# The first feed-forward's last output phase in three sweeps, and the next layer's token norm by halves

## The chip, the cores and the metric

The kernel runs on one core of a Trainium2 chip. The metric is the device time of one execution in microseconds, the median of several runs. The engines are named as in the profile: PE (TensorE, matmuls; PEld is its weight load), DVE (VectorE), ACT (ScalarE), POOL (GpSimd) and SP (SyncE, which issues most of the DMAs here). Each engine takes its instructions in the order in which they are written down for it.

## The reference, cut to what matters

Two layers act on 512 latent tokens and 256 context tokens of width 1024, all in fp32. Layer 0 is windowed attention and a SwiGLU feed-forward, layer 1 is retention and a feed-forward. Every mixer and every feed-forward stands behind an RMS norm whose result is scaled and shifted by numbers made from a condition vector, one set for the latent tokens and one for the context:

```
def rms_norm(x, g):
    y = xf * lax.rsqrt(jnp.mean(xf * xf, axis=-1, keepdims=True) + EPS)
    return y * g
def modulate(h, shift, scale):
    return h * (1 + scale) + shift
def swiglu(h, w_in, w_out):
    gate, up = jnp.split(h @ w_in, 2, axis=-1)
    return (jax.nn.silu(gate) * up) @ w_out

for i in range(DEPTH):                      # i = 0: attention, i = 1: retention
    h_x = modulate(rms_norm(x, norm1_g[i]), mx[0], mx[1])
    h_c = modulate(rms_norm(y_ctx, norm1_g[i]), mc[0], mc[1])
    ...                                     # the mixer, x = x + mx[2] * out_x, likewise y_ctx
    x = x + mx[5] * swiglu(modulate(rms_norm(x, norm2_g[i]), mx[3], mx[4]), ffn_w_in[i], ffn_w_out[i])
    ...                                     # likewise y_ctx with mc, in layer 0
```

The change lies where layer 0 ends and layer 1 begins: the last part of `swiglu(...) @ w_out` with its gated residual for both streams, the sums of squares of the new `x` and `y_ctx`, and `rms_norm` and `modulate` of layer 1's mixer. The hidden width of the feed-forward is 2816, that is 22 tiles of 128.

## The kernel before, in words

Activations lie with the 1024 features on the partitions, in eight tiles of 128, and tokens along the free dimension: `xr[d]` is the latent residual (128 x 512), `cres[d]` the context's (128 x 256). A matmul with a weight is done in three: weight and activation are each split into a rounded upper part and the rest (`split`, lines 164 to 166, and `next_w`, lines 136 to 142: ACT casts the upper part, DVE subtracts it for the lower), and `mm3` (lines 144 to 150) adds upper x upper, lower x upper and upper x lower in PSUM.

**The feed-forward of layer 0.** The 22 hidden tiles come in groups of 2, 4, 4, 4, 4 and 4. From the third tile on `seven` (line 1025) makes a tile by seven block products (line 908, `product`) of 12 matmuls each on sums of quarters of weights and activations: DVE forms the quarter sums of the weight pair `g`, `u` (lines 1031 to 1037), and the weights `b11`, `t1`, `b24` and `b3` are split from them. The products go to PSUM banks X, Y and Z in the order b11, b11, b24, t1, b3, b3, b24. Four of them use bank Y one after another, and ACT copies the first three out (lines 1046, 1051, 1055) before the next one on Y may start. After the first tile of a group, `output` (line 1078) multiplies the group before with its output weights: for a group of four there are four weights of 128 x 1024, each for two of the eight feature tiles `d`.

**The last output phase** is `output(prev, True)` (line 1156). It runs in two sweeps over `d`: first all eight for the latent tokens (banks `pj`, 512 columns, 12 matmuls each), then all eight for the context (bank Z, 256 columns). The four output weights stay in place for both. After each `d` comes the gated residual on DVE (`gated_add`, line 253) and the square (ACT, line 209) added to the running sum of squares (line 210, on DVE for the latent tokens, on POOL for the context). In the second `d` of the context sweep `rms(0)` (line 213) makes the latent statistics: a product with a matrix of ones (line 217), logarithm, exponential and square on ACT (lines 101, 196), two instructions on DVE (lines 197, 198).

**The start of retention.** `latent_norm` (line 1224) forms the normed and scaled latent tokens from whole rows of 512 (line 1229, DVE), and from them the upper (ACT, line 1232) and lower part (DVE, line 1233): for the feature tiles 0 to 3 only the first 256 tokens, for 4 to 7 all 512. The first value weights of head 0 are split between the two calls (lines 1326 to 1328). Then come the first value products (`values_first`, line 1266), the context statistics and norm (`context_norm`), the other value products, and `token_sums` (lines 1202 to 1215), which forms sums and differences of quarters of the normed latent tokens (`sA`) for the query, key and gate products. Before those, the key and query weights of head 0 are combined (lines 1374 to 1378) and split. The first query product is `product_q` on `sA` (line 1253).

**What sets the order.** The kernel is written as one stream of calls. A scheduler distributes it to the engines and puts each engine's instructions into one fixed order, from its own estimate of their times. Weight buffers come from pools: `w_raw` takes a raw weight from DRAM into one of two shared rooms or, by `raw_turn`, every third one into a room of the feed-forward's own pool. `w_parts` (line 126) hands out the rooms of the split weights in turn, two in the shared pool `rp` and one in the feed-forward's pool `fp`; the counter `wsel` says whose turn it is. A room is used again when its last reader is done, so the turn decides what a cast waits for. SP issues the weight loads in order, each when its room is free. In the last output phase weights one and two and the fourth take rooms by that turn from `rp`, `rp` and `fp`, and the third (`spare_w`) takes rooms that nothing else uses by then.

Of the kernel before, what the change touches and what calls it, by code (L numbers as in the profile page):

```python
# [8 lines left out]
F32 = mybir.dt.float32  # L9
# [40 lines left out]
def dit_kernel(ctx, tc, xT, cT, crow, small, consts, masks, tabs0, tabs1, jtab, adaQ, adaN, adaT, wst, out):  # L50
# [1015 lines left out]
    def square_and_stats(s, d, t):  # L1066
        add_square(s, d, t, eng=(nc.vector, nc.gpsimd)[s])
        if s == 1 and d == 1:
            ln_exp_turn()
            rms(0)  # L1070

# [6 lines left out]
    def output(acts, final):  # L1078
        gsz = len(acts)
        nd = 1024 // (gsz * P)  # L1080
        w = []

        def one(s, res, c, d):
            while len(w) * nd <= d:
                w.append(spare_w() if final and len(w) == 2 else next_w(fp, 1, raw_turn()))
            wd = w[d // nd]
            o = bank("Z")[:, 0:SC] if s else pj()
            for k in range(gsz):
                c0 = k * nd * P + (d % nd) * P
                mm3(o, (wd[0][:, c0:c0 + P], wd[1][:, c0:c0 + P]),  # L1090
                    (acts[k][:, c], acts[k][:, c.start + WIDE:c.stop + WIDE]), k == 0, k == gsz - 1)
            ins = gated_add(s, 0, 5, d, o, res)
            if cr and not final and s == 0 and d % 2:
                ada_next(ins)
            if final:
                square_and_stats(s, d, res[d])

        if final:
            for st in streams:
                for d in range(KT):  # L1100
                    one(*st, d)
        else:
            for d in range(KT):
                for st in streams:
                    one(*st, d)
# [23 lines left out]
    for gsz in FFN_GROUPS:  # L1129
        acts = []  # L1130
        for i in range(gsz):
# [4 lines left out]
            else:  # L1136
                if f == PLAIN:
                    last_sum()
                a, end = seven()
# [6 lines left out]
            if i == 0 and prev is not None:  # L1146
                output(prev, False)
# [7 lines left out]
    wsel[0] = 0  # L1155
    output(prev, True)
# [4 lines left out]
    for l, s, w in ((1, 0, 0), (1, 1, 0), (1, 0, 1)):  # L1161
        fold_gain(l, s, w)

# [60 lines left out]
    def latent_norm(ks, behind=()):  # L1224
        b, y = mods[1, 0], ssq[0]
        for k in ks:
            hm.append(t_qk(F32))
            t = hm[k]
            after(nc.vector.scalar_tensor_tensor(t, xr[k], acol[1, 0, 0][:, k:k + 1], y, mult, mult), behind)
            c = HALVES[0] if k < 4 else slice(0, SX)  # L1230
# [633 lines left out]
```

## Time and profile before

| | us |
|---|---|
| three runs | 1770.1, 1770.05, 1769.09 |
| their median | 1770.05 |
| the profiled execution | 1765.14 |
| its span, first to last instruction | 1763.4 |
| mean granted TensorE clock over the span | 0.996 of full speed |
| last output phase, latent sweep | about 858 to 881 of the span |
| last output phase, context sweep | about 881 to 893 |
| head 0 of retention up to its first query product | about 893 to 935 |

The span is what the views of the profile cover; the profiled execution's own time is 1.7 us more. The rows give the start in microseconds from the start of the span, the time, the engine, the line, the operation, and output and inputs with their shape; in square brackets stands the idle time before an instruction and what ended it. A row with a count (x3) is several instructions taken together, from the start of the first to the end of the last. Matmuls overlap, so their pace is the distance from one start to the next and not the time of one.

### The profile page before, as it was taken

Reading aid. Unit: us, or ns where it says so; the run is one execution under the profiler, and the core shown is the slowest. Engines: PE = TensorE matmul, PEld = TensorE weight load, DVE = VectorE, ACT = ScalarE, POOL = GpSimd, SP = SyncE. Lnnn points to the kernel's source line nnn. Section 1 sums busy time; section 2 is a strip of 40 time slices with the busy share of each in tenths; the row PEclk is TensorE's granted clock in tenths of the full one; section 3 lists DMA queues with packets and bytes.
Section 4 is the critical chain, followed back from the end, with each engine's and each line's share of the span. In section 5 each row is a group of like instructions: output and inputs, shape, how many; then the busy total and the mean of one; then the engine's idle time right before and its main releaser. Section 6 shows DMA issues by size and latency. Waiting matters only on the chain.

```text
span 1763.4 us, 27889 instructions
## 1 busy us (share of the span) xinstructions
PE 1716.5 (97%) x10984; PEld 1531.5 (87%) x10984; DVE 1332.7 (76%) x2342; ACT 841.3 (48%) x1487; POOL 122.4 (7%) x267
## 2 busy tenths in 40 slices
PE   6999999999999999999998999999999999999999
PEld 4788787889999999999887888898897889989998
DVE  6687786478778787877799758758767897777774
ACT  5467786364434333343464534524534565345442
POOL 0014344000000000000010000000000100000000
PEclk9999999999999999999999999999999999999999
DMA  9510014133243434343333434434433323233322
GB/s 345 232 49 14 15 58 157 49 127 113 96 132 122 142 120 155 108 145 130 96 133 120 157 98 132 155 108 133 146 105 108 96 93 111 85 108 108 97 83 84
DMA packets 60899, 205.65 MB, mean 117 GB/s; under 512 B 6752, under 2 KB 7136, under 8 KB 60640
## 3 DMA queue, kind: packets, MB, share of 16 engines
q1 hardware_dynamic: 53856, 178.71, 30.5%
q0 software_dynamic: 6912, 25.17, 4.5%
q8 instruction: 86, 1.41, 0.3%
q14 instruction: 45, 0.37, 0.1%
HBM read 201.75 MB, written 2.10 MB: 116 GB/s over the span
## 4 chain that ended last, share of the span: by engine, by line
PE 78%; DVE 12%; DMA 5%; ACT 3%; issue 1%; POOL 0%; SPq 0%; DVEq 0%; ACTq 0%; POOLq 0%
PE Y L908 14%; PE Z L908 7%; PE pj L150 7%; PE pj L149 7%; PE pj L148 7%; DMA wraw<-in_wst_dram 4%; PE X L908 3%; PE Y L1253 3%; PE Z L1266 3%; DVE wlo L166 3%; PE pO L732 2%; PE pT L704 2%; PE S L684 2%; PE pj L1266 2%; PE X L1253 1%
## 5 line engine op out<-in xcount | busy, mean ns | idle before, releaser
L165 ACT CAST whi<-wraw 128x1024 fp32r<-128x1024 f32 x177 | 185.5, 1051 | 305.2 <-PE Z L150 71.5
L166 DVE TENSOR_TENSOR wlo<-wraw,whi 128x1024 fp32r<-128x1024 f32 x177 | 216.1, 1223 | 39.4 <-ACT whi L165 38.9
L908 PE MATMUL Y<-aq,whi 128*128 128x384 f32 x640 | 173.9, 335 | 0.4 <-ACT hn L1046 0.3
L253 DVE SCALAR_TENSOR_TENSOR res<-pj,mod,res 128x512 f32<-128x512 f32 (+1 forms) x110 | 80.4, 732 | 81.2 <-PE pj L150 80.1
L141 DVE TENSOR_TENSOR wlo<-wraw,whi 128x1024 fp32r<-128x1024 f32 x79 | 96.5, 1223 | 35.2 <-ACT whi L140 34.6
L140 ACT CAST whi<-wraw 128x1024 fp32r<-128x1024 f32 x79 | 82.9, 1049 | 77.1 <-PE Z L150 24.3
L908 PEld LDWEIGHTS Y<-aq,whi 128*128 128x128 f32 x640 | 116.7, 188 | 1.8 <-ACT hn L1046 1.4
L908 PE MATMUL Y<-aq,wlo 128*128 128x384 f32 x320 | 107.0, 334 | 0.0
L271 DVE CUSTOM_DVE_ANT_0 y<-adaw,crow,small_sb 128x1024 bf16<-128x1024 f32 x64 | 81.9, 1280 | 32.9 <-DMA adaw<-in_adaT_dram 32.7
L1266 PE MATMUL Z<-whi,sA 128*128 128x512 f32 x256 | 81.0, 392 | 1.4 <-ACT whi L165 1.4
L101 ACT ACTIVATE pr<-pr,stat,qs 128x513 f32<-128x513 f32 (+2 forms) x96 | 74.2, 775 | 12.4 <-DVE stat L691 9.7
L698 POOL TENSOR_SCALAR pr<-pr,stat 128x512 f32<-128x512 f32 (+2 forms) x96 | 65.3, 693 | 76.6 <-DVE stat L695 57.7
L148 PE MATMUL pj<-ax,whi 128*128 128x512 f32 x176 | 68.7, 390 | 1.2 <-DVE res L253 1.2
L150 PE MATMUL pj<-ax,whi 128*128 128x512 f32 x176 | 68.7, 390 | 0.0
L149 PE MATMUL pj<-ax,wlo 128*128 128x512 f32 x176 | 68.5, 389 | 0.0
L148 PE MATMUL pj<-act,whi 128*128 128x512 f32 x168 | 66.0, 393 | 0.0
L149 PE MATMUL pj<-act,wlo 128*128 128x512 f32 x168 | 65.9, 392 | 0.0
L150 PE MATMUL pj<-act,whi 128*128 128x512 f32 x168 | 65.5, 390 | 0.0
L268 POOL DMA_DIRECT2D adaw<-in_adaT_dram x48 | 25.6, 533 | 514.6 <-DVE mod L271 420.1
L908 PE MATMUL Y<-sA,whi 128*128 128x256 f32 x304 | 60.8, 282 | 0.0
L908 PEld LDWEIGHTS Y<-aq,wlo 128*128 128x128 f32 x320 | 60.1, 188 | 0.0
L685 DVE CUSTOM_DVE_ANT_0 pr<-S,mask,qs 128x256 f32<-128x256 f32 (+1 forms) x96 | 52.5, 568 | 8.4 <-PE S L684 5.1
(545 smaller groups left out, 5227.8 us busy)
## 6 DMA issues: line engine op xcount, KB each, us to landing
wraw<-in_wst_dram SPq DMA_DIRECT2D x238, 512.0 KB, 3.6
adaw<-in_adaT_dram POOLq DMA_DIRECT2D x48, 512.0 KB, 3.8
wx<-in_wst_dram SPq DMA_DIRECT2D x24, 512.0 KB, 4.9
adan<-in_adaQ_dram SPq DMA_DIRECT2D x16, 512.0 KB, 8.4
adan<-in_adaN_dram SPq DMA_DIRECT2D x16, 512.0 KB, 7.5
res<-in_xT_dram SPq DMA_DIRECT2D x16, 256.0 KB, 4.4
q<-in_adaN_dram SPq DMA_DIRECT2D x16, 256.0 KB, 3.2
aq<-in_adaN_dram SPq DMA_DIRECT2D x12, 256.0 KB, 5.9
```

The lines of the kernel that those rows point to most:

```text
L101: ins = nc.scalar.activation(*args, **kw)
L140: nc.scalar.copy(hi, raw)
L141: nc.vector.tensor_tensor(lo, raw, hi, op=sub)
L148: nc.tensor.matmul(o, whi, xhi, start=first, stop=False)
L149: nc.tensor.matmul(o, wlo, xhi, start=False, stop=False)
L150: return nc.tensor.matmul(o, whi, xlo, start=False, stop=last)
L165: nc.scalar.copy(hi, t)
L166: return nc.vector.tensor_tensor(lo, t, hi, op=sub)
L253: return nc.vector.scalar_tensor_tensor(res[d], o, mods[l, s][:, part, d:d + 1], res[d], mult, add)
L271: after(nc.vector.tensor_tensor_reduce(junk, w, cr[:, s * 1024:(s + 1) * 1024], 1.0, sm_t[:, C_ADAB + l * 48 + j:C_ADAB + l * 48 + j + 1], ...
L908: nc.tensor.matmul(o, p, r, start=first and k + i == 0, stop=k == 3 and i == 2, skip_group_check=not first)
L1266: ins = nc.tensor.matmul(o, p, r, start=first and k + i == 0, stop=k == 3 and i == 2, skip_group_check=not first)
```

## The change

The last output phase goes over the eight feature tiles three times instead of twice: the first 256 latent tokens, the other 256, then the context. Each sweep has its own statistics: those of the first half are made in the second sweep, those of the second half in the third. The squares of the first half are added on DVE, all others on POOL. Each product of a sweep has 256 columns, and the products alternate between the banks `pj` and Z.

The four output weights take other rooms. The first comes by the turn, which is set so that it gets the room of the feed-forward's own pool; the second and third lie in halves in eight rooms `aq` that held the upper activations of the feed-forward (`token_room_w`); the fourth is `spare_w`. So that the turn comes out like this, `wsel` is set to 2 ahead of the last hidden tile and again ahead of the last output phase. The last hidden tile's own weights thereby change rooms too: b11 gets the room in `fp`, which the tile before used for b3, and b24 and b3 get the rooms in `rp`. The two rooms in `rp` are then free for retention's first value weights while the sweeps run.

The latent norm of retention works on halves: both calls at its old place do the first 256 tokens of all feature tiles, and a third call, ahead of `token_sums`, does the other 256, with the upper and lower part for the tiles 4 to 7.

```diff
+    def token_room_w():
+        raw, w = raw_turn(), ([], [])
+        for c in range(2):
+            hi, lo = (T(ep, 768, "aq", 8, F32R)[:, 0:512] for _ in range(2))
+            split(raw[:, 512 * c:512 * c + 512], hi, lo)
+            w[0].append(hi)
+            w[1].append(lo)
+        return w
...
-        if final:
-            for st in streams:
-                for d in range(KT):
-                    one(*st, d)
...
+    def last_output(acts):
+        w = []
+        for s, res, c, part in ((0, xr, HALVES[0], HALVES[0]), (0, xr, HALVES[1], HALVES[1]),
+                                (1, cres, slice(SX, WIDE), slice(0, SC))):
             for d in range(KT):
+                if len(w) * 2 <= d:
+                    w.append((lambda: next_w(fp, 1, raw_turn()), token_room_w, token_room_w, spare_w)[len(w)]())
+                o = bank("Z")[:, 0:SC] if d % 2 else pj(SC)
+                out_products(o, w[d // 2], d % 2 * P, acts, c, 2 * P)
+                nc.vector.scalar_tensor_tensor(res[d][:, part], o, mods[0, s][:, 5, d:d + 1], res[d][:, part],
+                                               mult, add)
+                first = s == 0 and c.start == 0
+                add_square(s, d, res[d], part, eng=nc.vector if first else nc.gpsimd, fresh=first or s == 1)
+                if not first and d == 1:
+                    if s == 0:
+                        ln_exp_turn()
+                    rms(0, HALVES[s])
...
                 if f == PLAIN:
                     last_sum()
+                if f == FT - 1:
+                    wsel[0] = 2
                 a, end = seven()
...
-    wsel[0] = 0
-    output(prev, True)
+    wsel[0] = 2
+    last_output(prev)
     F.close()
     E.close()
...
+    wsel[0] = 0
...
-    def latent_norm(ks, behind=()):
-        b, y = mods[1, 0], ssq[0]
+    def latent_norm(ks, half, behind=()):
+        b, y, c = mods[1, 0], ssq[0], HALVES[half]
         for k in ks:
-            hm.append(t_qk(F32))
-            t = hm[k]
-            after(nc.vector.scalar_tensor_tensor(t, xr[k], acol[1, 0, 0][:, k:k + 1], y, mult, mult), behind)
-            c = HALVES[0] if k < 4 else slice(0, SX)
-            hi, lo = first_quarters(k, 0) if k < 4 else h_rest[k - 4]
-            nc.scalar.activation(hi, t[:, c], AF.Identity, bias=b[:, 0, k:k + 1])
-            nc.vector.scalar_tensor_tensor(lo, t[:, c], b[:, 0, k:k + 1], hi, add, sub)
+            if not half:
+                hm.append(t_qk(F32))
+            t = hm[k][:, c]
+            after(nc.vector.scalar_tensor_tensor(t, xr[k][:, c], acol[1, 0, 0][:, k:k + 1], y[:, c], mult, mult), behind)
+            if k < 4 and half:
+                continue
+            hi, lo = first_quarters(k, half)
+            nc.scalar.activation(hi, t, AF.Identity, bias=b[:, 0, k:k + 1])
+            nc.vector.scalar_tensor_tensor(lo, t, b[:, 0, k:k + 1], hi, add, sub)
...
-    latent_norm(range(4))
+    latent_norm(range(4), 0)
     b11 = first_weights_v(0)
-    latent_norm(range(4, KT), [last_split[0]])
+    latent_norm(range(4, KT), 0, [last_split[0]])
...
         if hd == 0:
+            latent_norm(range(KT), 1)
             sums = token_sums(hm, 0, T(qp, 64, "sh2", 1), h_sum, [normed])
```

More of the change, by code (lines that the diff above doesn't have):

```diff
@@ L1064, in dit_kernel @@
     streams = ((0, xr, slice(0, SX)), (1, cres, slice(SX, WIDE)))
[L1066 to L1070, printed above, removed]
     def spare_w():
@@ L1146, in dit_kernel @@
             if i == 0 and prev is not None:
-                output(prev, False)
+                output(prev)
             f += 1
```

35 lines of the change are left out of this document (16 added, 19 removed).

## The prediction

> **What bounds the kernel now.** I read the page first (span, busy shares, the chain that ended last), then the stages around the change, then PE's waits there, then single rows.
>
> ```profile
> span 1763.4 us, 27889 instructions
> PE 1716.5 (97%) x10984; PEld 1531.5 (87%) x10984; DVE 1332.7 (76%) x2342; ACT 841.3 (48%) x1487; POOL 122.4 (7%) x267
> PE 78%; DVE 12%; DMA 5%; ACT 3%; issue 1%; POOL 0%; SPq 0%; DVEq 0%; ACTq 0%; POOLq 0%
> ```
>
> TensorE is busy 97% of the span and holds 78% of the chain, so work added to PE costs its full time, and work moved off another engine pays only where PE waits. The stages, in windows of time (columns: us; busy time and count of PE, PEld, DVE, ACT, POOL; clock; DMA share; GB/s):
>
> ```profile
> 858.00:881.00 23.00, 23.00 (x105) 18.93 (x105) 16.73 (x26) 8.93 (x13) 0.00 (x0) 1.00 0.20 66
> 881.00:893.00 12.00, 11.86 (x94) 11.18 (x93) 9.81 (x16) 7.96 (x15) 4.45 (x5) 1.00 0.28 95
> 893.00:897.00 4.00, 1.47 (x7) 0.79 (x6) 4.00 (x8) 2.18 (x4) 2.41 (x2) 1.00 0.42 131
> 897.00:931.00 34.00, 33.65 (x192) 28.95 (x190) 33.60 (x66) 21.59 (x40) 0.07 (x1) 1.00 0.39 126
> 931.00:935.00 4.00, 0.92 (x5) 0.72 (x6) 4.00 (x6) 2.35 (x4) 0.00 (x0) 1.00 0.28 112
> 935.00:939.00 4.00, 4.00 (x22) 3.89 (x21) 2.89 (x4) 1.99 (x2) 0.00 (x0) 0.57 0.30 82
> ```
>
> 858 to 881 is the latent output sweep: PE full, VectorE with 6.3 us free. 881 to 893 is the context sweep. From 893 VectorE is full for 42 us and PE waits for it twice; after the second wait the granted clock is 0.57 for 4 us, about 1.7 us of PE lost. PE's waits in this stretch:
>
> ```profile
> PE Z L1266 <- ACT whi L165: 3.1, 2, 1.6
> PE Y L1253 <- ACT whi L165: 1.9, 1, 1.9
> PE Y L1253 <- DVE wlo L166: 1.5, 1, 1.5
> PE Z L1266 <- DVE wlo L166: 1.4, 2, 0.9
> ```
>
> At 893 the first value product waits 1.6 + 0.9 = 2.5 us for its weights, whose casts and lower parts stand behind the token norm. At 931 the first query product waits 1.9 + 1.5 = 3.4 us. So the change can win at most 2.5 + 3.4 + 1.7 = 7.6 us here, and a few tenths of waits beyond.
>
> **The change, part by part.**
>
> *Narrower products.* The latent sweep's 96 matmuls of 512 columns become 192 of 256. Their pace is in these rows, 24 matmuls each (first and last of the group):
>
> ```profile
> 869.47 0.39 PE L148 MATMUL pj<-act,wraw 128*128 128x512 f32 x1
> 874.68 0.39 PE L150 MATMUL pj<-act,wraw 128*128 128x512 f32 x1
> 886.96 0.28 PE L148 MATMUL Z<-act,wraw 128*128 128x256 f32 x1
> 889.72 0.28 PE L150 MATMUL Z<-act,wraw 128*128 128x256 f32 x1
> ```
>
> 23 steps take 5.21 us at 512 (0.2265 each) and 2.76 us at 256 (0.120). 192 x 0.120 - 96 x 0.2265 = **+1.3 us**, all on PE. The Trainium skill ("TensorE: Matmul & The Clock Gate", "Back-to-back issue gap") puts the isolated warm step at N/2.4 + 2.5 ns, so it would make this 96 x (2 x 109.2 - 215.8) ns = +0.25 us, an estimate. The trace's 0.120 is above that rule's 0.109, and the row decides.
>
> *Statistics.* One product with the ones matrix of 512 columns becomes two of 256.
>
> ```profile
> 883.22 1.02 PE L217 MATMUL pj<-y,ones_sb 128*128 128x512 f32 x2
> 884.21 0.28 PE L149 MATMUL Z<-act,wlo 128*128 128x256 f32 x1
> 901.66 0.60 PE L217 MATMUL pj<-y,ones_sb 128*128 128x256 f32 x2
> 902.52 0.50 PE L1266 MATMUL X<-wlo,aq 128*128 128x512 f32 x1
> ```
>
> Start to the second matmul behind it is 0.99 us (0.12 of it the product after) and 0.86 us (0.23): 0.87 against 2 x 0.63, **+0.4 us**. In the written order each stands 24 matmuls (2.9 us) behind the last product whose square it needs, so I add nothing for waiting (bounds 0 and 0.7 us each).
>
> *VectorE, ScalarE, POOL.* By the written orders VectorE gets 24 instructions more, ScalarE 17, POOL 7. Half rows against whole:
>
> ```profile
> 893.33 0.86 DVE L1233 SCALAR_TENSOR_TENSOR aq<-qk,mod,aq 128x256 fp32r<-128x256 f32 x2
> 897.27 2.07 DVE L1229 SCALAR_TENSOR_TENSOR qk<-res,acol,y 128x512 f32<-128x512 f32 x3
> ```
>
> A half costs about 0.39 us, a whole about 0.66. Gated adds and norm products, 16 each instead of 8: 2 x 8 x (0.78 - 0.66) = +1.9; four upper tiles' lower parts halved, +0.5; seven whole adds of squares (0.6) become halves on VectorE (0.34) and halves on POOL: -1.8; together about +0.6. The 6.3 us free in the latent sweep cover it, and the norm's first half moves there too. Without that cover the 0.6 would stand in the full stretch from 893.
>
> *First value weights.* The last output weights no longer sit in the shared pool, so the two first value weights are cast and split during the sweeps, as is the norm of the first half. The wait of 2.5 us at 893 goes: **-2.5 us**. Late next there is nothing: the second pair's lower parts stand right behind the last gated add, and five microseconds of products cover them (24 x 0.2265).
>
> *Last hidden tile.* To leave that pool free, the tile's first weight (b11) moves to the single buffer that the tile before still reads with its second-last product.
>
> ```profile
> 841.56 1.06 ACT L165 CAST whi<-wraw 128x1024 fp32r<-128x1024 f32 x1 [1.54 <-PE Z L908]
> 842.25 0.69 DVE L1033 TENSOR_TENSOR wraw<-wraw 128x512 f32<-128x512 f32 x1
> 844.64 1.22 DVE L166 TENSOR_TENSOR wlo<-wraw,whi 128x1024 fp32r<-128x1024 f32 x1
> 848.32 1.28 DVE L271 CUSTOM_DVE_ANT_0 y<-adaw,crow,small_sb 128x1024 bf16<-128x1024 f32 x1
> 852.10 0.33 PE L908 MATMUL Y<-aq,whi 128*128 128x384 f32 x1
> 854.18 0.33 PE L908 MATMUL Z<-aq,whi 128*128 128x384 f32 x1
> 854.44 0.48 ACT L1055 COPY sq<-Y 128x384 f32<-128x384 f32 x1 [1.66 <-PE Y L908]
> wraw<-in_wst_dram SPq DMA_DIRECT2D x238, 512.0 KB, 3.6
> ```
>
> A product of `seven` is 2.08 us (from 852.10 to 854.18). b11 is free when the product read at 841.56 ends; cast and lower part end at 841.6 + 1.06 + 1.22 = 843.9, one product later PE wants it at 843.5: 0.4 us. The written order then fills PE with early output products, whose weight's lower part stands on VectorE behind the quarter sums and a reduction (1.28): ten instructions, five of the 0.69 kind, four shorter and the reduction, 6.3 us by my estimate; it ends near 843.9 + 6.3 + 1.2 = 851.4, PE is there at 843.9 + 3 x 2.08 + 0.2 = 850.4: 1.0 us. Third, ScalarE's copy of the third Y product (the row at 854.44) now stands behind casts of output weights two and three. Those loads start when their rooms fall free, near 852.7 and 853.8, and land 3.6 us later, the second perhaps 4.6 as two share the queue: 858.4, cast 0.6, copy 0.5, so PE has its last product at 859.5 instead of 858.9: 0.6 us. Sum **+2.0 us**; bounds 0 (all three covered, as now) and 5 (below). On SP no load is added; the value weights' loads only move ahead.
>
> PE is then +1.3 + 0.4 + 2.0 - 2.5 = +1.2 us at the context statistics.
>
> *Behind the context statistics.* This part decides, since VectorE takes its work in order.
>
> ```profile
> 902.88 0.45 ACT L101 ACTIVATE y<-pj,small_sb 128x256 f32<-128x256 f32 x1
> 903.81 0.42 ACT L196 ACTIVATE sq<-y 128x256 f32<-128x256 f32 x1
> 904.84 0.42 DVE L197 SCALAR_TENSOR_TENSOR sq<-pj,sq 128x256 f32<-128x256 f32 x1
> 930.24 1.23 DVE L1375 TENSOR_TENSOR wraw<-wx,wraw 128x1024 f32<-128x1024 f32 x1
> 933.20 1.22 DVE L166 TENSOR_TENSOR wlo<-wraw,whi 128x1024 fp32r<-128x1024 f32 x1
> ```
>
> The statistics product starts at 901.66 and ends near 902.3; ScalarE takes it up at 902.88 (0.5 us late), VectorE at 904.84 (0.6 late). Changed, both are idle by then: **-1.1 us**. But the written order keeps L197 ahead of everything that follows, so VectorE, finished with the latent norm near 900, only waits. From L197 to the end of the query weight's lower part is 29.6 us now (904.84 to 934.4); the changed order puts another weight's lower part (1.14 us start to start) ahead of it: **+1.1 us**. PE's product at 931 thus comes at +1.2 - 1.1 + 1.1 = **+1.2 us**, waits about 3.4 us as before, and the clock drop follows as before. The later heads keep PE's order; about ten of some 120 VectorE instructions in a head change places, which I price at 0, bounds -1 and +1.
>
> Sum: 1765.14 us of the profiled execution (span 1763.4 and 1.7 around it) becomes 1766.3. The median of the runs shown is 1770.05, 4.9 above that execution; the same difference gives **1771.2 us**. A difference of 0.2% (3.5 us) is about what a measurement of this kernel can tell from no change.
>
> **Rivals.**
>
> *The head start survives* (faster). If VectorE comes to the query weight 3 us or more sooner, the wait of 3.4 us ends and the clock stays full: PE goes on at its own time, 1.2 us late, so 1.2 - 3.4 - 1.7 = -3.9, about 1766. For it: about 10 us of the norm that VectorE now does from 893 to 905 is done before the sweeps end. Against it: L197. The Trainium skill (same page, "What's actually happening") says the clock halves after an idle window of about 3.4 us. The waits at 931 with one matmul between them, followed by 0.57, agree with it. By that rule a wait a little shorter than now already keeps the clock.
>
> ```profile
> adan<-in_adaQ_dram SPq DMA_DIRECT2D x16, 512.0 KB, 8.4
> ```
>
> *The copy waits for loads* (slower). If the landing behind the ScalarE casts takes 8.4 us instead of 4.6, PE stands 3.8 us more: +5.0, about 1775. It decides from 7 us of landing. For it: three loads fall due within 2 us, and a group of loads of the same size does take that long; against it: weights land in 3.6 us by the median.
>
> *POOL holds VectorE* (slower). Seven more POOL adds run in the second sweep, beside the norm.
>
> ```profile
> 888.40 0.74 POOL L210 TENSOR_TENSOR y<-y,sq 128x256 f32<-128x256 f32 x1 [0.58 <-ACT sq L209]
> 888.44 1.24 DVE L1229 SCALAR_TENSOR_TENSOR qk<-res,acol,y 128x512 f32<-128x512 f32 x1
> 890.00 0.74 DVE L1229 SCALAR_TENSOR_TENSOR qk<-res,acol,y 128x512 f32<-128x512 f32 x1
> ```
>
> Beside an add the norm product takes 1.24 us, alone 0.74: 0.5 us. 7 x 0.5 = 3.5 us at most; I took none, as the sweep has cover. If VectorE is full there and PE waits for banks, +1.2 + 3.5 = +4.7, about 1775. The Trainium skill ("SBUF — State Buffer", "Who interferes with whom") says a VectorE instruction with two SBUF inputs and a POOL instruction that reads SBUF block each other wholly. The 0.5 us above agrees; a whole add each time would be 7 x 0.74 = 5.2 us.
>
> **How the numbers follow.** Forecast 0.36 (own range 1768 to 1773.5), head start 0.34, loads 0.16, POOL 0.14. Range 1763.5 to 1778. The low end is the head start with the last tile's waits at 0 (1766.2 - 2.0) and 0.7 for reordering; the high end is the loads' 1775 with 0.7 of waiting at each of the two statistics, 1 for reordering and 0.6 for VectorE's added work without cover. Faster by over 0.2% 0.34, within 0.36, slower 0.30.
>
> **What would show it.** Right: no wait at the first value product; 0.120 us per half product; waits of about 2 us in all in the last hidden tile; VectorE idle some 4 us ahead of L197; the query product's wait still above 3 us and a clock near 0.57 behind it. Wrong: that wait gone; PE waiting inside the sweeps; a long idle of ScalarE ahead of the output weights' casts.

## The result, and the profile after

| kernel | median, us | ratio to before, 95% interval |
|---|---|---|
| before (22 runs) | 1768.95 | |
| changed (22 runs) | 1772.87 | 1.002 [1.0012, 1.0028] |

The change costs 3.9 us, 0.2%; forecast were 1.2 us on the profiled execution (1766.3) and 1771.2 us for the median. Of the changed kernel 1773.63 us were profiled, of before 1765.14: these two differ by 8.5 us, more than twice what the medians do, since before's profiled execution lies 3.8 us under its median. So what is read from the two traces is read as places and causes; what it is worth is taken from the runs of the experiments.

The page of the changed kernel: span, busy shares, and the chain that ended last.

```profile
span 1771.6 us, 28136 instructions
PE 1722.1 (97%) x11082; PEld 1540.6 (87%) x11082; DVE 1335.4 (75%) x2366; ACT 845.1 (48%) x1504; POOL 128.1 (7%) x274
PE 74%; DVE 14%; DMA 6%; ACT 3%; issue 2%; POOL 0%; SPq 0%; DVEq 0%; ACTq 0%; POOLq 0%
```

PE gave up 4 points of the chain, to DVE and DMA (2 and 1) and to issue (1), so a good part of what was lost is waiting. PE's busy time rose too, by 5.6 us: the products are narrower, and more of them run at half clock (last section). The stages after (columns: us; busy time and count of PE, PEld, DVE, ACT, POOL; clock; DMA share; GB/s):

```profile
858.00:881.00 23.00, 22.65 (x172) 21.91 (x171) 19.74 (x41) 14.18 (x27) 1.86 (x2) 1.00 0.39 128
881.00:893.00 12.00, 10.79 (x89) 10.53 (x88) 11.24 (x23) 7.74 (x19) 4.85 (x8) 1.00 0.01 5
893.00:897.00 4.00, 4.00 (x36) 4.00 (x35) 4.00 (x9) 0.57 (x2) 1.54 (x2) 1.00 0.47 152
897.00:904.30 7.30, 7.30 (x41) 6.35 (x40) 7.30 (x14) 6.15 (x12) 3.94 (x4) 1.00 0.25 80
904.30:913.40 9.10, 7.21 (x32) 5.63 (x30) 4.65 (x10) 3.09 (x7) 0.00 (x0) 1.00 0.79 280
```

PE is now full from 893 to 904.3, where it stood 2.5 us before. But there are two new gaps: 1.2 us in the second sweep (881 to 893), and 1.9 us behind the context statistics (904.3 to 913.4), in a stretch in which DVE, full before, works for half the time. PE's waits, 835 to 985 (us in total, times, longest):

```profile
PE Y L1272 <- DVE wlo L166: 2.3, 1, 2.3
PE pj L1285 <- DVE hc L243: 1.9, 1, 1.9
PE Z L1285 <- ACT gate L1442: 1.9, 1, 1.9
PE Z L1285 <- ACT whi L165: 1.6, 1, 1.6
PE pj L217 <- POOL y L210: 1.2, 1, 1.2
PE Y L1272 <- ACT whi L165: 1.1, 1, 1.1
PE pj L149 <- DVE wlo L141: 0.9, 1, 0.9
PE Y L908 <- ACT sq L1055: 0.3, 1, 0.3
PE pj L1285 <- ACT hc L242: 0.3, 1, 0.3
PE Y L908 <- DVE wlo L166: 0.3, 1, 0.3
```

The first query product (Y L1272) waits 2.3 + 1.1 = 3.4 us, as before. The rows L149 and L908 are the last hidden tile, 1.5 us in all. The waits of Z L1285 for `gate` and `whi` (1.9 and 1.6) lie behind the query products, where before has 1.9 and 1.4. Not forecast were the 1.9 + 0.3 us of pj L1285, the context's tiles, and the 1.2 us of pj L217, the statistics. First the former, in rows (SP's are the DMA issues):

```profile
903.07 2.01 SPq L1198 DMA_DIRECT2D wraw<-in_wst_dram  x2
905.13 1.37 SPq L1198 DMA_DIRECT2D wx<-in_wst_dram  x3
911.78 1.22 DVE L1394 TENSOR_TENSOR wx<-wx 128x1024 f32<-128x1024 f32 x1 [2.88 <-DMA wx<-in_wst_dram]
913.45 0.63 PE L1285 MATMUL pj<-whi,hc 128*128 128x512 f32 x1 [1.94 <-DVE hc L243]
938.09 0.39 PE L1272 MATMUL Y<-sA,whi 128*128 128x256 f32 x1 [1.11 <-ACT whi L165]
```

L1394 subtracts the raw query weights q22 and q12. It stands in DVE's list among the context's norm tiles. q22's load is the first of the three at 905.13, and SP takes it up only after two loads into `wraw`, those of the first key weights, whose rooms come free when DVE has made the lower parts of the second pair of value weights. It goes out as third of five loads within some 3 us, and DVE can use it 6.65 us later (911.78), where loads into `wx` take 4.4 us by the median of this page. DVE stands 2.88 us, and behind it the context's tiles, for which PE waits.

In before the same subtraction (L1374) waits for nothing, because SP has another order there: both raw query weights are loaded by the `wx` rows at 893.30 and 896.88, ahead of the two key weights at 902.49.

```profile
893.30 0.33 SPq L1181 DMA_DIRECT2D wx<-in_wst_dram  x1
896.88 0.91 SPq L1181 DMA_DIRECT2D wx<-in_wst_dram  x2
902.49 2.13 SPq L1181 DMA_DIRECT2D wraw<-in_wst_dram  x2
905.25 1.22 DVE L1374 TENSOR_TENSOR wx<-wx 128x1024 f32<-128x1024 f32 x1
```

So the change not only moved loads ahead: in the new order q22's load fell behind the key weights' loads, and so behind rooms that DVE frees late.

Now the statistics of the second half. POOL's adds and the instructions of DVE beside them:

```profile
889.67 0.70 PE L217 MATMUL pj<-y,ones_sb 128*128 128x256 f32 x2 [1.21 <-POOL y L210]
884.01 1.75 DVE L1247 SCALAR_TENSOR_TENSOR qk<-res,acol,y 128x256 f32<-128x256 f32 x2
896.74 0.86 DVE L1247 SCALAR_TENSOR_TENSOR qk<-res,acol,y 128x256 f32<-128x256 f32 x2
901.83 2.90 DVE L166 TENSOR_TENSOR wlo<-wraw,whi 128x1024 fp32r<-128x1024 f32 x2
902.07 1.57 POOL L210 TENSOR_TENSOR y<-y,sq 128x256 f32<-128x256 f32 x1 [0.51 <-ACT sq L209]
```

Two half norm products, 0.86 us undisturbed (896.74), take 1.75 beside POOL's adds. The two lower parts that free the `wraw` rooms take 2.90 us instead of 2.3, beside an add that itself takes 1.57 instead of 0.74.

The first query product of before, for comparison:

```profile
932.61 0.39 PE L1253 MATMUL Y<-sA,whi 128*128 128x256 f32 x1 [1.93 <-ACT whi L165]
```

How much later the changed kernel is than before, at the same matmul of both traces (start of after minus start of before): 0.6 us just before the last hidden tile begins, 2.4 just after it, 904.31 - 901.66 = 2.65 at the context statistics, 938.09 - 932.61 = 5.5 at the first query product, 6.0 to 7.1 in the later heads, 9.2 from 1390 on, 8.2 at the end.

### The profile page after: what moved, and what is told of

The parts are those of the page before. It is cut to its first block, busy times and chain, and to the rows that moved or that the text cites. A ratio compares the mean times of both kernels' runs of the same rounds, so it can differ in the third digit from the quotient of the medians.

```text
span 1771.6 us, 28136 instructions
## 1 busy us (share of the span) xinstructions
PE 1722.1 (97%) x11082; PEld 1540.6 (87%) x11082; DVE 1335.4 (75%) x2366; ACT 845.1 (48%) x1504; POOL 128.1 (7%) x274
## 4 chain that ended last, share of the span: by engine, by line
PE 74%; DVE 14%; DMA 6%; ACT 3%; issue 2%; POOL 0%; SPq 0%; DVEq 0%; ACTq 0%; POOLq 0%
PE Y L908 13%; PE Z L908 7%; PE pj L148 6%; PE pj L150 6%; PE pj L149 6%; DMA wraw<-in_wst_dram 4%; PE X L908 3%; DVE wlo L166 3%; PE Z L1285 3%; PE Y L1272 3%; PE pT L704 2%; PE pO L732 2%; PE S L684 2%; PE pj L1285 2%; PE X L1272 1%
## 5 line engine op out<-in xcount | busy, mean ns | idle before, releaser
L908 PE MATMUL Y<-aq,whi 128*128 128x384 f32 x640 | 174.0, 336 | 1.7 <-ACT hn L1046 1.3
L253 DVE SCALAR_TENSOR_TENSOR res<-pj,mod,res 128x512 f32<-128x512 f32 (+1 forms) x102 | 74.3, 729 | 78.4 <-PE pj L150 77.4
L908 PEld LDWEIGHTS Y<-aq,whi 128*128 128x128 f32 x640 | 116.6, 188 | 3.4 <-ACT hn L1046 2.2
L908 PE MATMUL Y<-aq,wlo 128*128 128x384 f32 x320 | 107.1, 335 | 0.3 <-DVE wlo L166 0.3
L1285 PE MATMUL Z<-whi,sA 128*128 128x512 f32 x256 | 81.0, 392 | 1.6 <-ACT whi L165 1.6
L149 PE MATMUL pj<-ax,wlo 128*128 128x512 f32 x176 | 68.5, 389 | 0.0
L149 PE MATMUL pj<-act,wlo 128*128 128x512 f32 (+1 forms) x156 | 60.0, 385 | 0.9 <-DVE wlo L141 0.9
L908 PE MATMUL Y<-sA,whi 128*128 128x256 f32 x304 | 60.7, 282 | 0.1
L908 PEld LDWEIGHTS Y<-aq,wlo 128*128 128x128 f32 x320 | 60.1, 188 | 0.6 <-DVE wlo L166 0.6
L148 PE MATMUL pj<-act,whi 128*128 128x512 f32 (+1 forms) x156 | 60.0, 385 | 0.0
L150 PE MATMUL pj<-act,whi 128*128 128x512 f32 (+1 forms) x156 | 59.6, 382 | 0.0
```

The source lines that it names most:

```text
L148: nc.tensor.matmul(o, whi, xhi, start=first, stop=False)
L149: nc.tensor.matmul(o, wlo, xhi, start=False, stop=False)
L150: return nc.tensor.matmul(o, whi, xlo, start=False, stop=last)
L253: return nc.vector.scalar_tensor_tensor(res[d], o, mods[l, s][:, part, d:d + 1], res[d], mult, add)
L908: nc.tensor.matmul(o, p, r, start=first and k + i == 0, stop=k == 3 and i == 2, skip_group_check=not first)
L1285: ins = nc.tensor.matmul(o, p, r, start=first and k + i == 0, stop=k == 3 and i == 2, skip_group_check=not first)
```

## The experiments

All edits are to the changed kernel unless the text says otherwise. Each was timed in five rounds on one chip together with the kernel before; the ratio is always to that. The groups ran on different chips, where before's median was 1768.18 (e1 to e4), 1768.13 (f1 to g1), 1769.32 (g2, h2, h3) and 1768.83 us (b1), and the changed kernel itself was timed only beside the 1768.95 above. So an edit is set against the changed kernel by what each loses to the before beside it: the changed kernel 3.9 us by medians, 1.0020 [1.0012, 1.0028] as a ratio.

| run | median, us | minus before's, us | ratio, 95% interval |
|---|---|---|---|
| e1: q12, q22 loaded first | 1773.72 | +5.5 | 1.0030 [1.0019, 1.0042] |
| e2: last tile's weight in the shared pool | 1776.54 | +8.4 | 1.0041 [1.0029, 1.0053] |
| e3: second half's adds on DVE | 1769.16 | +1.0 | 1.0005 [0.9996, 1.0014] |
| e4: e1 + e2 + e3 | 1773.49 | +5.3 | 1.0027 [1.0017, 1.0037] |
| f1: table, q12, q22 loaded first | 1770.07 | +1.9 | 1.0006 [0.9996, 1.0016] |
| f2: e3 + f1 | 1769.37 | +1.2 | 1.0005 [0.9996, 1.0013] |
| f4: all adds on DVE | 1769.06 | +0.9 | 1.0004 [0.9994, 1.0015] |
| g1, g2: one latent sweep, new rooms | 1770.51, 1770.84 | +2.4, +1.5 | 1.0009 [0.9999, 1.0019], 1.0007 [0.9997, 1.0016] |
| h2: f2 + query weights earlier on DVE | 1767.07 | -2.2 | 0.9985 [0.9975, 0.9994] |
| h3: as h2, no extra buffer | 1768.24 | -1.1 | 0.9992 [0.9983, 1.0001] |
| b1: kernel before + edits of h2 without e3 | 1767.05 | -1.8 | 0.9991 [0.9982, 1.0] |

**e1, the load of q22 alone.**

```diff
+        if hd == 0:
+            q12, q22 = chunk(bq + 2, True), chunk(bq + 3, True)
         k11, k21 = split_chunk(chunk(bq)), split_chunk(chunk(bq + 1))
```

> Edit to the changed kernel: in head 0 the loads of the two weights q12 and q22 are issued ahead of the first two key weights instead of behind them; nothing else moves. Theory L (the load is the loss): in the changed kernel VectorE stands 2.9 us for q22 behind the context statistics, TensorE waits 1.9 + 0.3 us for the context's tiles and runs at half clock for 3.4 us after that. Without it VectorE and what it feeds come 2.9 to 3.6 us sooner: 1772.9 - 3.6 = 1769.3 us, level with the kernel before, no wait at the context's products, one clock drop fewer. Rival N (narrower products, statistics and the last hidden tile are the loss, the waits behind only change places): the wait of 2.2 us goes but the first query product waits that much longer, the time stays at 1772.9 within 1 us.

Not faster: 1.0030. By the time alone theory L would be dead, and rival N, which forecast no gain, would be right. But N's own sign, a longer wait at the first query product, did not come (1.1 + 2.3 us as ever). The trace shows the same wait at the context's tiles with another cause:

```profile
913.16 0.71 ACT L101 ACTIVATE dx<-rj,dcol 128x384 f32<-128x384 f32 x1 [2.91 <-DMA rj<-in_jtab_dram]
915.13 0.80 PE L1285 MATMUL pj<-whi,hc 128*128 128x512 f32 x1 [2.40 <-ACT hc L242]
```

DVE's stand is gone, but now the distance table `rj` is the load behind the two `wraw`, ScalarE's list stands for it, and the context's upper parts stand behind that. The edit passed the wait from one engine in order to another. It tests nothing of theory L; f1 does.

**e2, the last hidden tile.**

```diff
-                if f == FT - 1:
-                    wsel[0] = 2
```

> Edit to the changed kernel: the last hidden tile's first weight stays in the shared pool, as in the kernel before; sweeps and norm are as changed. Theory T (the tile's room costs): the three waits in the last hidden tile, 0.27 + 0.86 + 0.33 = 1.5 us, go. If they reach the end, 1771.4 us. Theory L (the stand for q22's load sets what follows): TensorE comes 1.5 us sooner to the sweeps, but VectorE's stand ends when the load lands, so TensorE waits up to 1.5 us longer at the context's tiles: 1772.9 within 0.5. Rival R (the room was needed): the first value weights come into a pool that is still read, and the wait of the kernel before, 2.5 us at the first value product, is back: 1774 or more.

Slower than the changed kernel, 1.0041. No wait at the first value product came back, so rival R is wrong in its mechanism. Theory T is wrong too: the tile has a longer wait of another kind.

```profile
854.14 0.62 ACT L165 CAST aq<-wraw 128x512 fp32r<-128x512 f32 x1 [2.75 <-DMA wraw<-in_wst_dram]
854.67 0.47 ACT L1051 COPY hn<-Y 128x384 f32<-128x384 f32 x1
855.19 0.44 PE L908 MATMUL Y<-aq,whi 128*128 128x384 f32 x1 [2.18 <-ACT hn L1051]
```

ScalarE stands for a load of an output weight, and the copy that frees PE's bank stands behind the cast. The granted clock is 0.5 for 3.4 us right after. This is the prediction's rival of the copy that waits for loads; it was not in the changed kernel (0.33 us there) but lies one edit away.

**e3, POOL's adds.**

```diff
-                add_square(s, d, res[d], part, eng=nc.vector if first else nc.gpsimd, fresh=first or s == 1)
+                add_square(s, d, res[d], part, eng=nc.gpsimd if s else nc.vector, fresh=first or s == 1)
```

> Edit to the changed kernel: the second half's adds of squares run on VectorE instead of POOL; the context's stay on POOL. Theory P (POOL's adds are part of the loss): the wait of 1.2 us at the second half's statistics goes, and the norm products beside the adds take 0.8 instead of up to 1.85 us for two: -1.2 us, 1771.7. Theory L: VectorE then comes sooner to the context statistics, or not at all since it gets eight adds of 0.34 us (2.7 us) more, but the stand for q22's load ends no sooner: 1772.9 within 0.5. Rival V (VectorE full): its 2.7 us more are not covered, the context's tiles and the first query weight come later by up to 2.7 us: up to 1775.6.

1769.16, 1.0 us above the before beside it where the changed kernel loses 3.9: a gain of 2.9 us (2.7 by the ratios), more than twice what theory P promised, and level with before.

```profile
886.06 0.59 PE L217 MATMUL pj<-y,ones_sb 128*128 128x256 f32 x2
899.58 1.21 DVE L166 TENSOR_TENSOR wlo<-wraw,whi 128x1024 fp32r<-128x1024 f32 x1
901.20 1.37 SPq L1198 DMA_DIRECT2D wx<-in_wst_dram  x3
906.41 1.23 DVE L1394 TENSOR_TENSOR wx<-wx 128x1024 f32<-128x1024 f32 x1 [0.97 <-DMA wx<-in_wst_dram]
```

No wait at the statistics; the second lower part undisturbed at 1.21 us; and q22's load, which leaves 0.4 us behind that lower part's end in both kernels, goes out earlier: at 901.20 against 905.13, of which 2.4 us lie between the two traces already before the last hidden tile, so 1.5 us are e3's. It also lands sooner, 5.2 us from issue to use instead of 6.65. DVE stands 0.97 us for it instead of 2.88. Counted at the same matmuls from the last hidden tile on, e3 gains 1.3 us at the statistics, 1.6 more at the context's tiles, and 0.8 where the half clock had been. DVE has more work than in the changed kernel and is done earlier. This speaks for P, but also for L, since the stand went as well.

**e4, the three edits together.**

> The three edits together (loads of q12 and q22 first, the last hidden tile's weight in the shared pool, the second half's adds on VectorE). Theories L, T and P all true and additive: -3.6 - 1.5 - 1.2 = -6.3, 1766.6 us, 2.4 us below the kernel before. If VectorE's list behind the context statistics is full and sets the first query product, T and P are swallowed by that wait: 1769. If only N holds: above 1771.

1773.49. It carries e1's fault (1.71 us of ScalarE's stand for the table, 2.3 us of PE's wait behind it) and e2's (1.05 us). Sums of single gains were no guide here.

**f1, the loads again, with the table.**

```diff
+        if hd == 0:
+            jt, q12, q22 = strip_table(), chunk(bq + 2, True), chunk(bq + 3, True)
         k11, k21 = split_chunk(chunk(bq)), split_chunk(chunk(bq + 1))
```

> Edit to the changed kernel: in head 0 the distance table (rj) and the weights q12 and q22 are loaded ahead of the first two key weights. In the run with q12 and q22 alone ahead, VectorE's stand for q22 was gone, but the table came last, ScalarE stood 2.9 us for it with the context's tiles behind it, and TensorE's wait was 2.4 us again. Theory L (an in-order engine standing for a late load behind the context statistics is worth the wait and the clock's half stretch): with both ahead the wait of 2.2 us and the half clock behind it go, 1772.9 - 3.6 = 1769.3 us. Rival P (POOL's adds are the loss, by holding VectorE; the load is late only because VectorE is): VectorE is as late as before, the gain comes back as a longer wait at the first query product; 1772.9 within 1 us.

1770.07, 1.9 us above the before beside it: a gain of 2.0 us on the changed kernel by medians, 2.5 by the ratios (1.0006 against 1.0020; the ends of the two intervals overlap, 1.0016 and 1.0012). So theory L holds without any change to the adds, as far as the times can tell; the trace is plainer. PE's waits from 885 to 945 in this run are these three, and no other:

```profile
PE Y L1272 <- DVE wlo L166: 2.3, 1, 2.3
PE pj L217 <- POOL y L210: 1.2, 1, 1.2
PE Y L1272 <- ACT whi L165: 1.1, 1, 1.1
```

The wait at POOL's add is still there, the context's is not. Against rival P: the first query product waits 3.4 us as ever, not longer. Behind that wait f1 is 1.5 us later than the kernel before (counted from the last hidden tile), the changed kernel 5.7.

**f2, both.**

> The second half's adds on VectorE, and the table, q12 and q22 loaded ahead of the first key weights. With the adds alone on VectorE the time was level with the kernel before; VectorE's stand for q22 was 0.97 us and TensorE's waits at the context's tiles 0.30 + 0.43 us. Theory L and P both: these 0.7 us go and the rest stays: 1769.2 - 0.7 = 1768.5 us. If the first query product's wait of 3.4 us, which VectorE's full list sets, falls by that 0.97 us and with it the clock's half stretch behind it: 1766. If the load's place no longer matters: 1769.2 within 0.4.

1769.37, by its ratio the same as either alone. In its trace neither wait is left, and it is level with before (+0.2 us) behind the context's products. So e3 and f1 are two ways of removing one loss, the stand behind the context statistics: e3 by making DVE, and with it the rooms and the load, earlier, f1 by taking the load out of that queue. The 1.2 us at the statistics that e3 removes besides cannot be told in the medians.

**f4, no add on POOL.**

> All adds of squares on VectorE, the context's too, none on POOL. It measures what an add on POOL costs the engine beside it. With the second half's adds alone moved, seven context adds stayed on POOL, and three norm products beside them took 1.85 us for about 1.26. Theory P in full (each add holds VectorE for about 0.45 us, more than the 0.34 it takes there): VectorE's list is no longer for it, 1769.2 - 0.8 = 1768.4. Rival V (VectorE is full from the context sweep on, and an add costs it 0.34 us on it but little beside it): seven adds, 2.4 us later at the context statistics' follow-up and at the first query product: 1771.5.

1769.06, level with e3. Seven adds more on DVE cost nothing measurable, and seven adds fewer on POOL brought nothing: neither rival V's loss of 2.4 us nor theory P's gain of 0.8 shows. The intervals leave about 1.8 us either way, so the times say only that the two prices are of one size; in the traces f4 is 0.6 us earlier than e3 at the first query product, counted from the last hidden tile.

**g1 and g2, the rooms without the third sweep.**

```diff
-        for s, res, c, part in ((0, xr, HALVES[0], HALVES[0]), (0, xr, HALVES[1], HALVES[1]),
-                                (1, cres, slice(SX, WIDE), slice(0, SC))):
+        for s, res, c, part in ((0, xr, slice(0, SX), slice(0, SX)), (1, cres, slice(SX, WIDE), slice(0, SC))):
```

> One part of the change alone: the new rooms for the last output weights (and for the last hidden tile), but the latent tokens in one sweep of 512 columns with whole squares on VectorE and one statistics product at the context's second tile, so no norm before the context sweep; the norm is written by halves as in the changed kernel. Against the kernel before: the tile's waits +1.5 to +2.0. Theory S (the rooms alone remove the 2.5 us at the first value product): 1769.0 + 1.5 - 2.5 = 1768 us, better than the changed kernel by the 1.7 of the narrower products and statistics and by POOL's 3.8. Rival H (the wait goes only because the first half's norm is done during the sweeps): the first value product waits again, now for its operands, 2 us or more: 1771 or more.

> The kernel with the new rooms and one latent sweep once more, for a profile that can be read: the profile of its first run was taken in an execution of 9439 us, five times as long as all others, and shows no wait. The times of the first run gave 1.0009. Theory S: no wait at the first value product for its weights, the last hidden tile's waits of about 1.5 us as in the changed kernel, and the loss against the kernel before (1.6 us) made of the tile and of what stands behind the context statistics. Rival H: a wait of 2 us or more at the first value product.

One execution of g1, the profiled one, took 9440.88 us, which nothing here explains; the others are as g2's. Theory S holds in its mechanism, though not in its time (1768 forecast): with whole rows and no norm ahead of the context sweep the first value product does not wait, so the 2.5 us are the rooms' doing, not the halves'. Counted from the last hidden tile, this kernel is 1.4 us earlier than before at the context statistics. It gives that back, and more, at the query weight:

```profile
PE Y L1269 <- ACT whi L165: 4.6, 1, 4.6
PE Y L1269 <- DVE wlo L166: 1.4, 1, 1.4
```

6.0 us where before waits 3.4, and 6.8 us of half clock; behind the wait it is 3.4 us later than before. DVE has no head start here, makes the norm by halves (2 x 0.39 us against 0.66), and is busy without a stop from 893 to 940 (46.97 of 47 us): what PE gains ahead of DVE turns into waiting for it.

**h2 and h3, the order on DVE ahead of the query product.** In the changed kernel the weight of the first query product is added up and split at the end of DVE's list, and between its sum and its own lower part stand another lower part, a difference and a copy's lower part (2.6 us) that the product does not need. h2 puts the sum and the split ahead of the last pair of token sums:

```diff
+        def first_query():
+            r11, r21 = chunk(bq), chunk(bq + 1)
+            nc.vector.tensor_tensor(q12, q22, q12, op=sub)
+            done = nc.vector.tensor_tensor(r11, q12, r11, op=add)
+            query.extend((r11, r21, split_chunk(r11)))
+            return done
...
-            sums = token_sums(hm, 0, T(qp, 64, "sh2", 1), h_sum, [normed])
+            sums = token_sums(hm, 0, T(qp, 64, "sh2", 1), h_sum, [normed], first_query)
...
+            r1 = T(qw, 1024, "wx", 4)
+            nc.vector.tensor_tensor(r1, q22, k11, op=sub)
+            w1 = split_chunk(r1)
```

> To the kernel with the second half's adds on VectorE and the table, q12 and q22 loaded first: in head 0 the first query weight's sum and its lower part stand on VectorE ahead of the last pair of token sums, and the second query weight's ahead of w4's difference (it is written to a buffer of its own). Theory W (the wait at the first query product, 1.1 + 2.3 us, is VectorE's order, 2.6 us of work standing ahead that the product does not need): the wait falls below 1 us and the clock's half stretch behind it (1.7 us) goes: 1769.4 - 2.6 - 1.7 = 1765 us, below the kernel before. Rival M (the work is only moved): the next product waits instead, for its own weight, or for a load whose buffer the extra tile has taken: 1769 within 1 us.

> As the run before it, but without the extra buffer: w4's difference too stands ahead of the last pair of token sums, so that the second query weight can be written in place; VectorE ends the sums 1.1 us later. Theory W: waits of about 0.6 us at the first and 1.3 us at the second query product, no half clock: 1769.4 - 1.5 - 1.7 = 1766 us. Rival M: as above, 1769 within 1 us.

h2 is faster than before by 0.15%, 0.9985 [0.9975, 0.9994]; h3 lies between (0.9992) and its interval takes in 1: its first two query products wait 1.1 us for the sums and 1.6 us for a copy on ScalarE (0.6 and 1.3 were forecast), and a half clock follows all the same. h2's waits of PE:

```profile
PE Z L1287 <- DVE wlo L166: 3.4, 2, 2.3
PE Z L1287 <- ACT whi L165: 2.6, 1, 2.6
PE Y L1274 <- ACT whi L165: 0.9, 1, 0.9
```

The first query product starts without a wait, the second waits 0.9 us, and no half clock follows: theory W. PE is 3.3 us earlier than before there, counted from the last hidden tile. Then the gate weights' products wait 3.4 + 2.6 = 6.0 us for weights that DVE makes later (it stands only 0.3 us for a load there, so the extra buffer is hardly the cause), with 6.8 us of half clock behind: rival M, one stage on. About 2 us of gain are left in the medians; the two traces do not show them, since h2 ends 1.1 us later than before's profiled execution, counted in the same way.

**b1, the same edits on the kernel before.**

> The kernel before, without the three sweeps and the new rooms, with the same edits to loads and query weights as in the run that came out below it (table, q12 and q22 loaded early; the first query weight's sum and lower part ahead of the last pair of token sums; the second query weight's ahead of w4's difference). It asks whether that gain needs the change. Theory A (the gain is VectorE's order at the query weights alone, and the sweeps bring nothing): 0.9985 again, 1766.5 us. Rival C (in the kernel before VectorE is full from 893 on and has no room for it; the change's head start is what is spent): the wait of 3.4 us at the first query product becomes one at the sums or further on, 1769 within 1 us.

1767.05, 0.9991 [0.9982, 1.0]: 1.8 us under the before beside it, where h2 has 2.2. The two intervals overlap; they leave h2 up to 0.25% faster than b1 or 0.12% slower. b1's query products wait 1.1 + 0.9 us, and the gate weights' product 3.6 us, as in h2 one stage on. So no measurement here shows that the gain of h2 needs the three sweeps; rival C's wait came, but did not eat the gain.

## Why the prediction was right or wrong

- *Narrower products, +1.3.* Right. The step in the third group is 0.120 us (895.96 to 898.72 is 23 steps in 2.76 us).
- *Statistics, +0.4, and "I add nothing for waiting (bounds 0 and 0.7 us each)".* Wrong: 1.21 us at the second half's. The 2.9 us of products ahead of the statistics did not cover it: the last gated add came late on a DVE held by POOL's adds (a norm product of 0.96 us stands just ahead of it), and the square and its add on POOL (0.72 us) follow only then. In e3, with those adds on DVE, the wait is 0.
- *DVE +0.6 us, covered.* The cover was counted without POOL. In 881 to 893 DVE is busy for 11.24 of 12 us, and PE waits 1.2; in e3 it is busy for 11.83, and PE waits for nothing. So it was not the added work that broke the cover.
- *First value weights, -2.5.* Right. And g2 shows that the rooms alone do it.
- *Last hidden tile, +2.0.* Measured 0.27 + 0.86 + 0.33 = 1.5 us of waits (0.4, 1.0 and 0.6 forecast), and 1.8 us between the traces. Mechanism and order right.
- *PE +1.2 at the context statistics.* 2.65 - 0.58 = 2.1 measured: the wait of 1.21 at the statistics is in it, and 0.3 less elsewhere.
- *Context statistics -1.1.* Right in kind: the product starts at 904.31, and DVE stands 1.31 us ahead of L197, finished with its norm as foreseen, but by less (some 4 us were forecast).
- *Behind the context statistics, +1.2 and "on SP no load is added; the value weights' loads only move ahead".* This is the step that failed. It is true that none is added, but they do not only move ahead: q22's load fell behind the two key weights' loads (905.13 behind 903.07, in before 896.88 ahead of 902.49). DVE's list from L197 to the end of the query weight's lower part was taken as 29.6 + 1.1 = 30.7 us of work; it is 34.3 (906.43 to 940.70), because it held one instruction that waits for a load, and that load waits in SP's queue for rooms that DVE itself frees late. Cost: 2.88 us on DVE, 1.9 + 0.3 us on PE, and 3.4 us at half clock, none of which has a term in the sum. f1 shows the size of the error: with the load moved the same stretch is 30.1 us (910.68 to 940.81), PE is 1.5 us late at the query product (1.2 forecast), and the ratio of 1.0006 to before's 1768.13 us is +1.1 us (-0.7 to +2.8; the medians differ by 1.9).
- *The query product still waits about 3.4 us and the clock drops behind it.* Right, to 0.02 us (1.11 + 2.28 against 1.93 + 1.48). The head start did not survive, for the reason given, L197, and for one more: DVE's stand for q22's load behind it. The clock's part was read too strictly: the prediction sees the waits at 931 as agreeing with an idle window, but in before's window ahead of that drop (931.85 to 935.26) PE is busy for 1.18 of 3.41 us, so a wait a little shorter need not have kept the clock (last section).
- *Rival "POOL holds VectorE" (0.14).* Half true. The price per add is about right (0.5 us forecast, 0.49 in the rows of the last section), and e3 takes back most of the loss, but not by the route priced: PE does not wait for banks in the sweep, but at the statistics and, through the late rooms, for the load.
- *Rival "the copy waits for loads" (0.16).* Not in the changed kernel; found in e2.

So the change was forecast at +1.2 us and measured at +3.9. f1 takes back 2.0 to 2.5 of the 2.7 between them, within the noise of either. The absolute forecast, 1771.2, lies nearer to 1772.87 than that deserves, since it was put on a median of three runs, 1770.05, where 22 runs gave 1768.95: that nearness is luck. Why before's profiled execution lies 3.8 us under its own median is clear only in part. In all 13 traces PE runs the same matmuls up to the tile before the last hidden one, and the 12 other kernels come there between 1.8 us earlier and 4.9 us later than this execution, 1.8 later on average; where the rest comes from stays open.

## What to carry to other kernels

When work is moved ahead on an engine that takes its list in order, go through the list behind it and mark each instruction that waits for a load; then follow that load back through the issuing queue to the room it needs and to the instruction that frees the room. Here the loop closed on the same engine: DVE was late, so the room, so the queue, so the load for which DVE stood. Moving one load ahead of it only passed the wait to the next in the queue, until all that were needed early had gone. And when loads are moved ahead, compare the whole order of the issuing queue with the old one: a load that nobody touched can fall behind others.

## What the runs showed of the hardware

**The half clock comes in windows, and half a window's waiting is enough.** In the 13 traces (all but g1's), the stretches of granted clock 0.5 last 3.413 us or twice that (the last one of a trace is cut by the end of the program), and within a trace their starts lie whole multiples of 3.413 us apart (in after: 7, 21, 233, 8, 132 and 111 of them). So the time can be cut into such windows. From 800 us on, 31 half-clock stretches begin, the last one of each trace not counted; in the window ahead of each, PE was busy for 0 to 52% of the time. Of the windows without such a consequence the emptiest had 47, 47, 49 and 51%. Windows of after, before and after (clock in the third column from the right):

```profile
910.25:913.66 3.41, 1.47 (x7) 0.91 (x5) 1.88 (x3) 0.00 (x0) 0.00 (x0) 1.00 0.56 223
913.66:917.07 3.41, 3.10 (x7) 1.99 (x7) 3.31 (x8) 1.85 (x5) 0.00 (x0) 0.50 0.00 1
```

```profile
962.56:965.97 3.41, 1.62 (x8) 1.00 (x6) 3.41 (x6) 0.55 (x2) 0.00 (x0) 1.00 0.57 160
965.97:969.39 3.42, 3.33 (x15) 2.74 (x16) 2.92 (x5) 2.09 (x5) 0.00 (x0) 1.00 0.87 273
```

```profile
1388.12:1391.53 3.41, 1.44 (x11) 1.03 (x10) 2.03 (x4) 2.29 (x4) 0.00 (x0) 1.00 0.53 166
1391.53:1394.95 3.42, 3.07 (x14) 2.52 (x13) 2.38 (x4) 3.05 (x5) 0.00 (x0) 0.50 0.53 153
```

A wait of 1.88 us in before (962 to 966, PE busy for 1.62 of 3.41) cost nothing more; one of 1.97 in after (1.44 busy) was followed by two windows at half clock, 6.83 us; why a stretch lasts two windows and not one, with PE busy for 3.07 of 3.42 in the first, these traces do not tell. The Trainium skill ("TensorE: Matmul & The Clock Gate", "What's actually happening") gives a free-running window of 3413 ns, with which the distances agree; it asks for an idle window, and there the rows differ and decide: the windows ahead of these two drops were 43 and 42% busy. So a wait of some 2 us costs itself alone or a half-clock stretch besides, by where it falls in the window. It can be one reason why executions of one kernel differ: of the changed kernel's 22 runs the 16 with a mean clock of 0.992 to 0.995 take 1773.8 us on average, the 6 with 0.996 or 0.997 1769.5. It is not the only one, since within the first group the 3 runs at 0.993 and the 7 at 0.995 take the same (1773.8 and 1773.7).

**An add on POOL and a DVE instruction hold each other.** A 128x256 norm product takes 0.47 us alone (e3) and 0.96 beside an add (after, the rows below), two lower parts 2.90 instead of 2.3, and the add beside them 1.57 instead of 0.74. That the engines lock each other out in both directions agrees with the Trainium skill ("SBUF — State Buffer", "Who interferes with whom"). New to me was the price: 0.5 to 0.6 us of DVE where an add meets one of its instructions, against about 0.34 from start to start for the same add on DVE itself, so that moving adds from POOL to DVE cost nothing that f4 could measure.

```profile
897.17 0.47 DVE L1247 SCALAR_TENSOR_TENSOR qk<-res,acol,y 128x256 f32<-128x256 f32 x1
898.80 0.96 DVE L1247 SCALAR_TENSOR_TENSOR qk<-res,acol,y 128x256 f32<-128x256 f32 x1
```
